# The passage into the FFN: a norm's sum of squares taken from sums per column block, and turns by diagonals

## The chip, the cores and the metric

One core of one Trainium2 chip runs the whole layer. Its engines are TensorE (PE: matmuls, with PEld for its weight loads), VectorE (DVE), ScalarE (ACT), GpSimd (POOL) and SyncE (SP, which issues most of the DMAs). The metric is the device time of one launch in microseconds (us); the median of three runs before the change is 1506.01 us (1505.78 to 1507.14).

## The reference

One transformer layer over 256 latent tokens and 256 context tokens of width 2048: attention in two kinds, merged by gates and an output projection, then a gated FFN with a short convolution. Between the two halves stand two norms, and these are what the change is about:

```python
def rms_norm(x, g):
    y = x * lax.rsqrt(jnp.mean(jnp.square(x), axis=-1, keepdims=True) + EPS)
    return y * g

y, yc = mixer_sublayer(...)                   # ends in "@ w_o"
x = x + gt1 * rms_norm(y, g_attn_post)        # first norm, gain, residual
h = modulate(rms_norm(x, g_ffn_pre), sh2, sc2)  # second norm, scale and shift
x = x + gt2 * rms_norm(conv_ffn(h, w_up, conv_w, conv_b, w_down), g_ffn_post)
```

Write y for the projection times its gain row, r1 for the first norm's factor and x for the layer's input. The new x is x + r1 y. The second norm needs the sum of (x + r1 y)^2 over the 2048 columns of each token, which is also r1^2 sum(y^2) + 2 r1 sum(xy) + sum(x^2).

## The kernel before

Everything is f32; large matmuls are made of three products of a high and a low part. Weights come in blocks of 128 x 2048 f32 (1024 KB) into one of four buffers named raw; ACT writes the high part (wh, L137), DVE the low part (wl, L141), and `block(3)` asks for the next block's parts and for the loads of three blocks further on. The kernel is written with a planner that orders the instructions of each engine by its own estimates; `issue_after(i)` places an instruction behind i on i's engine, and inside `manual_schedule` PE's order is that of the text.

The output projection is `norm_gain`: four column blocks c of 512, each over 16 row tiles, for the two token tiles t = 0, 1 (L913). In each of the first three column blocks four weight blocks g serve both t; in the last one, t=0 finishes first and t=1 last, each over two blocks of weights. `close(t)` takes the sum of squares of a finished block on ACT (L922) and multiplies by the gain row `grow` on DVE (L923). `extra`, here `beside(c, g)`, loads x1 (the layer's input, one half per token tile) and runs `mods`, products of modulation weights (raw<-in_wm_b) with a row `crb` on DVE (L234).

After the last block, `done(t)`, here `residual(t)`, runs. `rstd_tok` makes r1 from the sums (L952 to L955). DVE then writes x1 = yg * r1 + x1 in four blocks (L1018), and ACT squares each of them to get the second norm's sum (L1028). For t=1 the last block goes over PE instead: x1 times the identity (L1009), then yg times a diagonal matrix of r1 (L1015), both into px, which ACT squares. The second `rstd_tok` gives the second norm's factor.

Then the turns: h2, the FFN's input, is needed with features on the partitions. `turn(b, ts)` turns groups of one or two 128-column tiles through PE: group 0 is tile 0, group 1 tiles 1 and 2, up to group 8, tile 15. For t=0 in groups 0 to 3 it multiplies x1 by a diagonal of the second norm's factor (L1055), which turns and scales in one; all others are transposes (L1057) of tiles scaled beforehand by `scaled` (L998 on ACT, L999 on DVE). `split_h2(b)` applies scale and shift and writes the high and low halves of h2 (L1072 to L1078). `keep_busy(n)` puts n products of the identity with itself on PE (L266) as padding. The first four products of the FFN, `first_pairs`, run row tile by row tile among the turns (L1091, L1093, then L204 and L205). At the end x1 is stored to DRAM (L1138) for the layer's last residual.

Of the kernel before, what the change touches and what calls it, by code (L numbers as in the profile page):

```python
# [13 lines left out]
ALU = mybir.AluOpType  # L14
# [54 lines left out]
def layer_kernel(ctx, tc, xc, xt, ccol, crow, wm_sc, wm_sd, wm_sh, wm_b, cols, wk, wkt, ws, rope, mask_a, bias_b, out):  # L69
# [8 lines left out]
    def acc(name):  # L78
        return ps.tile([P, 512], F32, tag="a", bufs=6, name=name)
# [817 lines left out]

    final = []

    def norm_gain(act, nk, yg, grow, ss, nm, lead, done, extra=None):  # L900


        for c in range(4):
            py = [acc(f"py_{nm}{c}_{t}") for t in range(2)]
            cs = slice(c * 512, c * 512 + 512)

            def part(wts, g, t):
                wh, wl = wts
                for kk in range(4):
                    k = 4 * g + kk  # L910
                    w = slice(kk * 512, kk * 512 + 512)
                    for q, (a, wt) in enumerate(((0, wh), (1, wh), (0, wl))):
                        p_ = nc.tensor.matmul(  # L913
                            py[t][:], act[:, k, a, t * P : t * P + P], wt[:, w],
                            start=k == 0 and q == 0, stop=k == nk - 1 and q == 2)
                final[:] = [p_.ins]

            def close(t, after=None):
                with ExitStack() as es:
                    if after:  # L920
                        es.enter_context(tc.issue_after(after))
                    nc.scalar.activation(yg[:, t, cs], py[t][:], AF.Square, accum_out=ss[:, t, c : c + 1])  # L922
                nc.vector.tensor_tensor(out=yg[:, t, cs], in0=py[t][:], in1=grow[:, cs], op=ALU.mult)  # L923

            n = nk // 4
            for g in range(n if c < 3 else n - lead):
                wts = block(3)
                for t in range(2):
                    part(wts, g, t)
                if extra:  # L930
                    extra(c, g)
            if c < 3:
                for t in range(2):
                    close(t)
                if c == 1:
                    warm_table(AF.Sqrt, nm, ss[:, 0, 0:1])
            else:
                wts, after = [], None
                for g in range(n - lead, n):
                    wts.append(block(3))  # L940
                    part(wts[-1], g, 0)
                for t in range(2):
                    if t:
                        for i, g in enumerate(range(n - lead, n)):
                            part(wts[i], g, 1)
                    close(t, after)
                    after = done(t)
        return after

    def rstd_tok(ss, r):  # L950

        nc.vector.tensor_reduce(out=r, in_=ss[:, :3], axis=mybir.AxisListType.X, op=ALU.add)  # L952
        nc.vector.tensor_scalar(out=r, in0=r, scalar1=1.0 / D, scalar2=EPS, op0=ALU.mult, op1=ALU.add)
        a_ = nc.scalar.activation(r, ss[:, 3:4], AF.Sqrt, scale=1.0 / D, bias=r)
        v_ = nc.vector.reciprocal(r, r)  # L955
        return a_.ins, v_.ins
# [5 lines left out]
    with ExitStack() as ys:  # L962
# [1 line left out]
        x1 = yp.tile([P, 2, D], F32, name="x1")  # L964

        def beside(c, g):
            if g == 2 and c in (1, 2):
                sync.dma_start(out=x1[:, c - 1], in_=xt[:, c - 1])
            if c < 3 and g:
                mods(1, crb[:], (c, g) != (2, 3))  # L970
            if (c, g) == (2, 3):
                nc.vector.tensor_tensor(
                    out=modx[:, 16:48], in0=modx[:, 16:48], in1=col[:, C_BMOD + 48 : C_BMOD + 80], op=ALU.add)
                nc.vector.scalar_tensor_tensor(
                    out=gcol[:, 1, :], in0=modx[:, 32:48], scalar=1.0, in1=col[:, C_GPRE2 : C_GPRE2 + KT],
                    op0=ALU.add, op1=ALU.mult)

        yg = yp.tile([P, 2, D], F32, name="yg")
        grow = yp.tile([P, D], F32, name="grow")
        ss = yp.tile([P, 2, 2, 4], F32, name="ss")  # L980
        r = yp.tile([P, 2, 52], F32, name="r")

        crb = silu_row(yp)
        gain_row(0, grow)
# [1 line left out]

        pu, dg = [], {}

        def diagonal(n, t):

            dg[n] = yp.tile([P, P], F32, name=f"dg{n}")
            return nc.scalar.activation(dg[n][:], ident[:], AF.Copy, scale=r[:, n, t : t + 1]).ins

        def scaled(t, c0, c1, act=False):

            cs, r_ = slice(c0 * P, c1 * P), r[:, 1, t : t + 1]
            if act:
                return nc.scalar.activation(yg[:, t, cs], x1[:, t, cs], AF.Copy, scale=r_).ins  # L998
            return nc.vector.tensor_scalar(out=yg[:, t, cs], in0=x1[:, t, cs], scalar1=r_, scalar2=None, op0=ALU.mult).ins  # L999

        def residual(t):
            rstd_tok(ss[:, 0, t], r[:, 0, t : t + 1])
            c3 = slice(1536, 2048)
            if t:

                pu.extend(acc(f"pu0_{i}") for i in range(4))
                px = pu[3]
                with tc.issue_after(final[0]):
                    p_ = nc.tensor.matmul(px[:], ident[:], x1[:, t, c3], start=True, stop=False).ins  # L1009
                with tc.issue_after(p_):  # L1010
                    b_ = keep_busy(4, "2", pu[0])
                with tc.issue_after(diagonal(0, t)):
                    diagonal(1, 0)
                with tc.issue_after(b_):
                    p_ = nc.tensor.matmul(px[:], dg[0][:], yg[:, t, c3], start=False, stop=True).ins  # L1015
            for c in range(3 if t else 4):
                cs = slice(c * 512, c * 512 + 512)
                v_ = nc.vector.scalar_tensor_tensor(  # L1018
                    out=x1[:, t, cs], in0=yg[:, t, cs], scalar=r[:, 0, t : t + 1], in1=x1[:, t, cs],
                    op0=ALU.mult, op1=ALU.add)  # L1020
                s_ = ss[:, 1, t, c : c + 1]
                if t and c == 2:
                    with tc.issue_after(v_.ins):
                        v_ = nc.vector.scalar_tensor_tensor(
                            out=yg[:, t, cs], in0=x1[:, t, cs], scalar=1.0, in1=x1[:, t, cs],
                            op0=ALU.mult, op1=ALU.mult, accum_out=s_)
                else:
                    a_ = nc.scalar.activation(yg[:, t, cs], x1[:, t, cs], AF.Square, accum_out=s_)  # L1028
                if t and c == 0:
                    with tc.issue_after(a_.ins):  # L1030
                        a_ = nc.scalar.activation(yg[:, t, c3], px[:], AF.Square, accum_out=ss[:, 1, t, 3:4])
            if t == 0:
                rstd_tok(ss[:, 1, t], r[:, 1, t : t + 1])
                return a_.ins
            with tc.issue_after(v_.ins), tc.issue_after(a_.ins):
                return p_, rstd_tok(ss[:, 1, t], r[:, 1, t : t + 1])[0]

        p_, q_ = norm_gain(zz, KT, yg, grow, ss[:, 0], "o", 2, residual, beside)
        zs.close()


# [3 lines left out]
        def turn(b, ts, js=None):  # L1045

            if b not in ptx:
                ptx[b] = (acc if b % 2 else bank)(f"ptx{b}")
            for t in ts:
                for f, j in enumerate(group[b]):  # L1050
                    if js and j not in js:
                        continue
                    d = ptx[b][:, f * S + t * P : f * S + t * P + P]
                    if t == 0 and b < 4:
                        nc.tensor.matmul(d, x1[:, t, j * P : j * P + P], dg[1][:], start=True, stop=True)  # L1055
                    else:
                        nc.tensor.transpose(d, yg[:, t, j * P : j * P + P], ident[:])  # L1057

        def split_h2(b):
            with ExitStack() as es:  # L1060
# [35 lines left out]
        with tc.issue_after(p_), tc.manual_schedule(engines={mybir.EngineType.PE}):  # L1096
            for b in range(4):
                turn(b, (0,))
            keep_busy(8, "3", pu[0])

            a_ = nc.scalar.activation(x1[:, 1, 1536:], pu[3][:], AF.Copy)
            with tc.issue_after(a_.ins), tc.issue_after(q_):
                scaled(0, 7, 8, True)
                scaled(0, 8, 12, True)
            scaled(1, 0, 1)
            scaled(1, 1, 4)
            scaled(1, 4, 8)
            behind[:] = [scaled(1, 8, 12)]
            turn(0, (1,))
            split_h2(0)  # L1110
            turn(1, (1,))
# [7 lines left out]
            turn(3, (1,))  # L1119
            first_pairs(1)  # L1120
            split_h2(3)
            with tc.issue_after(behind[0]):
                behind[0] = scaled(0, 12, 16, True)
            with tc.issue_after(behind[1]):
                behind[1] = scaled(1, 12, 16)
            for k in range(2, KT):
                if k % 4 == 0:
                    wh, wl = parts[nblk[0]]
# [342 lines left out]
```

## Time and profile before

| | |
|---|---|
| median of the runs | 1506.01 us (1505.78 to 1507.14) |
| the profiled execution | 1505.69 us |
| its span | 1503.90 us |
| mean granted clock of TensorE | 0.999 |
| PE busy | 1492.0 us (99%) |
| DVE busy | 1202.0 us (80%) |
| ACT busy | 800.7 us (53%) |
| output projection, PE's L913 | 678.4 to 765.6 us of the span |
| turns, PE's L1055 and L1057 | 768.6 to 792.5 us of the span |

The span runs from the first to the last instruction of the profiled execution; 1.79 us of its time lie around it. A chain row gives the start, the length and what ran; a timeline row gives the start, the length, the engine, the line, the operation with its tiles, how many rows were merged, and in brackets the idle time before it and what ended that. A row of groups gives the durations of one in ns. DMA rows give the size and the us from issue to landing. Durations of matmuls overlap, since they are pipelined; how much time they occupy on PE is read from start to start, or from the chain.

### The profile page before, as it was taken

What the parts mean: (1) busy time and instruction counts of PE and PEld (TensorE: products, weight loads), DVE (VectorE), ACT (ScalarE), POOL (GpSimd) and SP (SyncE); (2) the same over time, 40 slices, a digit from 0 to 9 for tenths busy, and PEclk for the clock granted to TensorE, in tenths of its full rate; (3) what the DMA queues carried; (4) which work ended last, traced back from release to release, by engine and by line L of the source; (5) the groups of instructions that cost most, each with busy time, mean ns of one, the idle gap of its engine ahead of it and who ended that gap; (6) DMA issues with size and microseconds to landing.
All of it is one profiled execution on the core that took longest, in us unless ns stands there. A gap on an engine that the chain in (4) does not pass through costs nothing.

```text
span 1503.9 us, 21730 instructions
## 1 busy us (share of the span) xinstructions
PE 1492.0 (99%) x8513; PEld 1282.2 (85%) x8513; DVE 1202.0 (80%) x1797; ACT 800.7 (53%) x1309; POOL 1.6 (0%) x10
## 2 busy tenths in 40 slices
PE   9999999999999999999999999999999999999997
PEld 7876889898888888888888888888888888888886
DVE  4496897999988888877678887887888878777776
ACT  4342532777764554454467555555555565455443
POOL 0000000000000000000000000000000000000000
PEclk9999999999999999999999999999999999999999
DMA  9988779754468888878846666666766655645653
GB/s 366 396 322 335 278 285 343 275 171 167 142 229 299 321 322 324 299 278 323 348 182 217 247 237 237 244 236 221 252 228 234 213 194 179 241 174 194 234 238 112
DMA packets 59254, 381.08 MB, mean 253 GB/s; under 512 B 6544, under 2 KB 6928, under 8 KB 17040
## 3 DMA queue, kind: packets, MB, share of 16 engines
q1 hardware_dynamic: 58432, 378.63, 67.8%
q8 instruction: 67, 1.10, 0.3%
q10 hardware_dynamic: 720, 1.07, 0.2%
q14 instruction: 35, 0.29, 0.1%
HBM read 375.43 MB, written 4.24 MB: 252 GB/s over the span
## 4 chain that ended last, share of the span: by engine, by line
PE 97%; DMA 1%; DVE 1%; ACT 1%; issue 0%; DVEq 0%; ACTq 0%
PE pu L204 21%; PE c L1256 13%; PE pu L205 11%; PE pv L686 7%; PE pg L204 7%; PE pk L468 7%; PE py_o L913 6%; PE pq L204 4%; PE pb L204 4%; PE pg L205 4%; PE pq L205 2%; PE x L1256 2%; PE pb L205 2%; PE po L823 1%; PE s L793 1%; PE pm L342 1%
## 5 line engine op out<-in xcount | busy, mean ns | idle before, releaser
L141 DVE TENSOR_TENSOR wl<-raw,wh 128x1024 fp32r<-128x1024 f32 (+1 forms) x444 | 523.4, 1207 | 141.4 <-ACT wh L137 141.1
L137 ACT ACTIVATE wh<-raw 128x1024 fp32r<-128x1024 f32 (+1 forms) x444 | 446.5, 1041 | 221.8 <-PE c L1256 58.3
L204 PE MATMUL pu<-h,wh 128*128 128x512 f32 x1404 | 488.1, 391 | 0.0
L205 PE MATMUL pu<-h,wl 128*128 128x256 f32 x1404 | 395.9, 282 | 0.0
L204 PEld LDWEIGHTS pu<-h,wh 128*128 128x128 f32 x1404 | 263.6, 188 | 55.6 <-issue 0.4
L205 PEld LDWEIGHTS pu<-h,wl 128*128 128x128 f32 x1404 | 265.4, 189 | 0.0
L204 PE MATMUL pg<-h,wh 128*128 128x512 f32 x464 | 161.5, 390 | 0.0
L1256 PE MATMUL c<-wh,ff 128*128 128x512 f32 x512 | 158.1, 389 | 0.0
L205 PE MATMUL pg<-h,wl 128*128 128x256 f32 x464 | 130.8, 282 | 0.0
L234 DVE SCALAR_TENSOR_TENSOR raw<-raw,crb 128x2048 f32<-128x2048 f32 x48 | 109.7, 2286 | 12.5 <-DMA raw<-in_wm_b_dram 11.9
L468 PE MATMUL pk<-h,ku 128*128 128x512 f32 x480 | 118.1, 398 | 0.9 <-DVE ku L141 0.4
L1256 PEld LDWEIGHTS c<-wh,ff 128*128 128x128 f32 x512 | 96.1, 188 | 19.8
L209 ACT ACTIVATE half_u<-pu 128x256 f32<-128x256 f32 x88 | 33.5, 382 | 147.2 <-PE pu L205 147.2
L468 PEld LDWEIGHTS pk<-h,ku 128*128 128x128 f32 x480 | 87.5, 188 | 25.6 <-issue 4.8
L204 PE MATMUL pq<-h,wh 128*128 128x512 f32 x304 | 108.6, 395 | 0.0
L204 PEld LDWEIGHTS pg<-h,wh 128*128 128x128 f32 x464 | 87.1, 188 | 18.2
L686 PE MATMUL pv<-wh,h 128*128 128x512 f32 (+1 forms) x384 | 101.7, 354 | 0.0
L1256 PE MATMUL c<-wl,ff 128*128 128x512 f32 x256 | 99.8, 390 | 0.0
L204 PE MATMUL pb<-h,wh 128*128 128x512 f32 x256 | 89.4, 390 | 0.0
L205 PEld LDWEIGHTS pg<-h,wl 128*128 128x128 f32 x464 | 87.7, 189 | 0.0
L205 PE MATMUL pq<-h,wl 128*128 128x256 f32 x304 | 85.5, 281 | 0.0
L913 PE MATMUL py_o<-wh,zz 128*128 128x512 f32 x256 | 78.7, 389 | 0.0
(229 smaller groups left out, 2009.2 us busy)
## 6 DMA issues: line engine op xcount, KB each, us to landing
raw<-in_ws_dram SPq DMA_DIRECT2D x222, 1024.0 KB, 4.9
raw<-in_wm_b_dram SPq DMA_DIRECT2D x64, 1024.0 KB, 4.9
raw<-in_wm_sc_dram SPq DMA_DIRECT2D x15, 1024.0 KB, 8.0
raw<-in_wm_sh_dram SPq DMA_DIRECT2D x16, 768.0 KB, 6.3
raw<-in_wkt_dram SPq DMA_DIRECT2D x10, 1024.0 KB, 6.3
raw<-in_wk_dram SPq DMA_DIRECT2D x7, 768.0 KB, 8.5
crb<-sild SPq DMA_DIRECT2D x4, 1024.0 KB, 7.9
sd<-in_wm_sd_dram SPq DMA_DIRECT2D x4, 1024.0 KB, 7.6
```

What stands on the lines that cost most here:

```text
L137: a_ = nc.scalar.activation(hi, src, AF.Copy)
L141: v_ = nc.vector.tensor_tensor(out=lo, in0=src, in1=hi, op=ALU.subtract)
L204: nc.tensor.matmul(pt[:, :], wh[:, w], a, start=first and i == 0, stop=False, skip_group_check=True)
L205: nc.tensor.matmul(pt[:, :S], wl[:, w], a[:, 0], start=False, stop=last and i == n - 1, skip_group_check=True)
L209: a_ = nc.scalar.activation(t[:], pt[:, S:], AF.Copy)
L234: nc.vector.scalar_tensor_tensor(out=r, in0=r, scalar=1.0, in1=row, op0=ALU.mult, op1=ALU.mult, accum_out=modx[:, j : j + 1])
L342: nc.tensor.matmul(pm[32 * j : 32 * j + 32, t * P : t * P + P], cc[:, q, :], rsc[k + t][:, q * P : q * P + P], start=q < 4, stop=q >= KT - ...
L468: nc.tensor.matmul(pk[:], wt[:, w], hh[:, :, k, a], start=k == 0 and a == 0 and wt is wh, stop=k == KT - 1 and a == 1)
L686: nc.tensor.matmul(pv[i][:, :nw], src[:, k, a, t0 : t0 + P], wt[:, w], start=k == 0 and q == 0, stop=k == KT - 1 and q == 2)
L793: nc.tensor.matmul(s_ps[:], qs[hd][:, a, qt * P : qt * P + P], k_, start=q == 0, stop=q == 2)
L913: p_ = nc.tensor.matmul(py[t][:], act[:, k, a, t * P : t * P + P], wt[:, w], start=k == 0 and q == 0, stop=k == nk - 1 and q == 2)
L1256: nc.tensor.matmul(pt[:], a(i), wt[:, w], start=k not in begun, stop=stop and q == 2, skip_group_check=True)
```

## The change

The second norm's sum is no longer taken from the finished x1. `norm_gain` gets a hook `more(c, t, cs)`, called for every closed block. Here it is `sums`: ACT squares yg (y in the text above) into a scratch tile with an accumulated sum, DVE multiplies yg, 2 and x1 with an accumulated sum, and for c = 0, 1, 2 ACT also squares one or two blocks of x1. x1 is therefore loaded in the first column block, at g = 0 and 1, not in the second and third.

`residual(t)` then adds up the three sums, combines them with r1 in two Horner steps, clamps at zero, and makes the factor with `rstd_of`. Between these it places the first part of x1 (columns 0 to 128), then the diagonal `dg[t]` on ACT, then columns 128 to 512, then column blocks 1 and 2 for t=0 and block 1 for t=1. The remaining blocks (t=1 block 2, t=0 block 3, t=1 block 3) come on DVE after the split of turn group 3.

All turns are products with the diagonal of their t. The tiles are no longer scaled beforehand; the products into px are gone; the padding is 24 calls in one place instead of 4 and 8.

```diff
@@ norm_gain
                 nc.vector.tensor_tensor(out=yg[:, t, cs], in0=py[t][:], in1=grow[:, cs], op=ALU.mult)
+                if more:
+                    more(c, t, cs)
@@ beside
-            if g == 2 and c in (1, 2):
-                sync.dma_start(out=x1[:, c - 1], in_=xt[:, c - 1])
+            if c == 0 and g < 2:
+                sync.dma_start(out=x1[:, g], in_=xt[:, g])
@@ new helpers
+        def squared(t, cs, c):
+            nc.scalar.activation(junk[:, 0], x1[:, t, cs], AF.Square, accum_out=sq[:, t, 2, c : c + 1])
+
+        def sums(c, t, cs):
+            nc.scalar.activation(junk[:, 0], yg[:, t, cs], AF.Square, accum_out=sq[:, t, 0, c : c + 1])
+            nc.vector.scalar_tensor_tensor(
+                out=junk[:, 1], in0=yg[:, t, cs], scalar=2.0, in1=x1[:, t, cs], op0=ALU.mult, op1=ALU.mult,
+                accum_out=sq[:, t, 1, c : c + 1])
+            for q in range(c, c + 1 + c // 2) if c < 3 else ():
+                squared(t, slice(q * 512, q * 512 + 512), q)
+
+        def residual_part(t, a, b):
+            cs = slice(a, b)
+            return nc.vector.scalar_tensor_tensor(
+                out=x1[:, t, cs], in0=yg[:, t, cs], scalar=r[:, 0, t : t + 1], in1=x1[:, t, cs],
+                op0=ALU.mult, op1=ALU.add).ins
@@ residual(t), new body
+            r1, v = r[:, 0, t : t + 1], m[:, t, 3:4]
+            rstd_tok(ss[:, t], r1)
+            nc.vector.tensor_reduce(out=m[:, t, :3], in_=sq[:, t], axis=mybir.AxisListType.X, op=ALU.add)
+            for q in (1, 2):
+                nc.vector.scalar_tensor_tensor(
+                    out=v, in0=m[:, t, 0:1] if q == 1 else v, scalar=r1, in1=m[:, t, q : q + 1], op0=ALU.mult, op1=ALU.add)
+            v_ = nc.vector.tensor_scalar(out=v, in0=v, scalar1=0.0, scalar2=None, op0=ALU.max)
+            with tc.issue_after(v_.ins):
+                v_ = residual_part(t, 0, P)
+            with tc.issue_after(v_):
+                v_ = rstd_of(v, r[:, 1, t : t + 1])
+            dg[t] = yp.tile([P, P], F32, name=f"dg{t}")
+            a_ = nc.scalar.activation(dg[t][:], ident[:], AF.Copy, scale=r[:, 1, t : t + 1]).ins
+            with tc.issue_after(v_):
+                v_ = residual_part(t, P, 512)
+            for c in range(1, 3 - t):
+                with tc.issue_after(v_):
+                    v_ = residual_part(t, c * 512, c * 512 + 512)
+            if t == 0:
+                return a_
+            return final[0], v_
@@ turn
-                    if t == 0 and b < 4:
-                        nc.tensor.matmul(d, x1[:, t, j * P : j * P + P], dg[1][:], start=True, stop=True)
-                    else:
-                        nc.tensor.transpose(d, yg[:, t, j * P : j * P + P], ident[:])
+                    nc.tensor.matmul(d, x1[:, t, j * P : j * P + P], dg[t][:], start=True, stop=True)
@@ the turns and first products
             for b in range(4):
                 turn(b, (0,))
-            keep_busy(8, "3", pu[0])
...
-            behind[:] = [scaled(1, 8, 12)]
+            pu.extend(acc(f"pu0_{i}") for i in range(4))
+            keep_busy(24, "3", pu[0])
+            behind[:] = [q_]
             turn(0, (1,))
             split_h2(0)
...
             split_h2(3)
-            with tc.issue_after(behind[0]):
-                behind[0] = scaled(0, 12, 16, True)
-            with tc.issue_after(behind[1]):
-                behind[1] = scaled(1, 12, 16)
+            for t, c in ((1, 2), (0, 3), (1, 3)):
+                with tc.issue_after(behind[1]):
+                    behind[1] = residual_part(t, c * 512, c * 512 + 512)
```

More of the change, by code (lines that the diff above doesn't have):

```diff
@@ L898, in layer_kernel, with norm_gain @@
     final = []
-    def norm_gain(act, nk, yg, grow, ss, nm, lead, done, extra=None):
+    def norm_gain(act, nk, yg, grow, ss, nm, lead, done, extra=None, more=None):
         for c in range(4):
@@ L979, in layer_kernel @@
         grow = yp.tile([P, D], F32, name="grow")
-        ss = yp.tile([P, 2, 2, 4], F32, name="ss")
-        r = yp.tile([P, 2, 52], F32, name="r")
+        ss = yp.tile([P, 2, 4], F32, name="ss")
+        sq = yp.tile([P, 2, 3, 4], F32, name="sq")
+        r = yp.tile([P, 2, 2], F32, name="r")
+        m = yp.tile([P, 2, 4], F32, name="m")
+        yp.tile([P, 72], F32, name="rim3")
+        junk = yp.tile([P, 2, 512], F32, name="junk2")
         crb = silu_row(yp)
@@ L987, in layer_kernel @@
         pu, dg = [], {}
[L989 to L999, printed above, removed]
@@ L1001, in residual @@
-        def residual(t):
[L1002 to L1026, printed above, removed]
-                else:
[L1028 to L1031, printed above, removed]
-            if t == 0:
[L1033 to L1036, printed above, removed]
@@ L1038, in layer_kernel @@
-        p_, q_ = norm_gain(zz, KT, yg, grow, ss[:, 0], "o", 2, residual, beside)
+        def squared(t, cs, c):
[7 more added lines that the diff above has]
+                squared(t, slice(q * 512, q * 512 + 512), q)
@@ L1039, in layer_kernel @@
+        p_, q_ = norm_gain(zz, KT, yg, grow, ss, "o", 2, residual, beside, sums)
         zs.close()
@@ L1053, in turn @@
                     d = ptx[b][:, f * S + t * P : f * S + t * P + P]
-                    if t == 0 and b < 4:
-                        nc.tensor.matmul(d, x1[:, t, j * P : j * P + P], dg[1][:], start=True, stop=True)
-                    else:
-                        nc.tensor.transpose(d, yg[:, t, j * P : j * P + P], ident[:])
+                    nc.tensor.matmul(d, x1[:, t, j * P : j * P + P], dg[t][:], start=True, stop=True)
         def split_h2(b):
@@ L1098, in layer_kernel @@
                 turn(b, (0,))
-            keep_busy(8, "3", pu[0])
[L1101 to L1107, printed above, removed]
-            behind[:] = [scaled(1, 8, 12)]
+            pu.extend(acc(f"pu0_{i}") for i in range(4))
+            keep_busy(24, "3", pu[0])
+            behind[:] = [q_]
             turn(0, (1,))
```

## The prediction

> **What bounds the kernel now.** I read the page's shares of the chain that ended last, then the engines in four stretches, then the waits of PE and its weight loads (PEld), then the chain through the passage.
>
> ```profile
> PE 97%; DMA 1%; DVE 1%; ACT 1%; issue 0%; DVEq 0%; ACTq 0%
> 678.00:765.60 87.60, 87.60 (x389) 72.61 (x388) 61.29 (x71) 42.16 (x61) 0.00 (x0) 1.00 0.84 325
> 765.60:775.00 9.40, 8.71 (x62) 7.32 (x62) 7.13 (x19) 6.74 (x18) 0.00 (x0) 1.00 0.50 209
> 775.00:796.00 21.00, 21.00 (x125) 18.24 (x125) 17.30 (x31) 15.35 (x26) 0.00 (x0) 1.00 0.38 138
> 796.00:1500.00 704.00, 700.12 (x3723) 606.01 (x3721) 557.30 (x782) 385.23 (x574) 0.00 (x0) 1.00 0.60 218
> PE pu L1091 <- ACT h L1073: 0.4, 1, 0.4
> PEld pu L204 <- ACT h L1073: 0.2, 1, 0.2
> ```
>
> PE is the bound: 97% of the chain. A windows row gives the stretch, its length, then busy time of PE, PEld, DVE, ACT, POOL, the granted clock and the DMA share. In the output projection (678 to 765.6) PE is never idle, so nothing that is done sooner there can shorten the run; it can only become late. In the passage (765.6 to 775) PE idles 0.7 us. The clock is 1.00 throughout. From 796 on it is busy 700.1 of 704 us, and the waits view names no engine that it waits for there. So the change is worth what it does to PE's own list of work and waits between 765.6 and about 796, and a slip there reaches the end whole.
>
> The chain through the passage (start, length, what):
>
> ```profile
> 754.94 10.67 PE py_o L913 x47
> 765.63 0.70 ACT yg L922 x2
> ...
> 766.96 0.16 DVE r L955
> 767.14 0.41 ACT dg L992
> 767.60 1.12 PE pu L1015 x2
> 768.72 1.56 PE ptx L1055 x14
> 770.29 1.79 PE pu L266 x16
> 772.07 0.12 PE ptx L1057
> 772.22 0.57 ACT h L1073
> ...
> 774.96 0.26 PE pu L204
> ...
> 780.67 0.44 PE ptx L1057 x4
> ```
>
> The projection ends at 765.61, the first turn of t=1 at 772.19, and its first h2 tile starts on ACT at 772.22. PE passes 16 records of padding (8 calls of keep_busy: **two records a call**) right up to that turn. The real rows L204 begin at 774.96.
>
> ```profile
> L1057 PE MATMUL ptx<-ident,yg x25: 270/272/273, 771.9 to 792.5; 128*128 128x128 f32 x25
> L1055 PE MATMUL ptx<-dg,x x14: 273/275/275, 768.6 to 770.0; 128*128 128x128 f32 x14
> ```
>
> The code makes 25 transposes and 7 products with a diagonal: a transpose is one record, a product two. By the chain, a transpose occupies 0.44/4 = 0.11 us and a product 1.56/7 = 0.223 us.
>
> **The change part by part.**
>
> *Turns.* All 32 turns become products: 25 x (0.223 - 0.11) = 25 x 0.113 = 2.8 us more PE work, beside nothing, since PE has no idle time there. The Trainium skill, page "TensorE: Matmul & The Clock Gate", section Terms, says against this change that transpose mode is 4x faster for FP32. By that a product would be 0.44 us, the 25 turns would cost 8.2 us, and my total below would be near 10 us; the x14 row, at twice a transpose, decides against the 4, and the case gets no chance: those seven products have the same tiles and form.
>
> *Padding.* What leaves PE: the identity and diagonal products into px (L1009, L1015) and 12 calls of padding. What comes: 24 calls, 48 records of 1.79/16 = 0.112 us, 5.37 us. PE's list is written out by hand, so from 765.61: seven products for t=0, 1.56, to 767.17; padding to 772.54; first turn of t=1, two records, to **772.76, against 772.19: +0.57**. The seven need t=0's diagonal and columns up to 896, which are made beside the last 5.4 us of projection; these rows of DVE show the room:
>
> ```profile
> 760.91 0.69 DVE L923 TENSOR_TENSOR yg<-py_o,grow 128x512 f32<-128x512 f32 x1 [2.93 <-ACT yg L922]
> 761.71 2.74 DVE L1018 SCALAR_TENSOR_TENSOR x<-yg,r,x 128x512 f32<-128x512 f32 x4
> 762.49 0.64 ACT L1028 ACTIVATE yg<-x 128x512 f32<-128x512 f32 x1 [1.29 <-DVE x L1018]
> 763.03 0.18 ACT L1028 ACTIVATION_READ_ACCUMULATOR yg<-x 128x1 f32 x1
> 764.57 0.15 DVE L952 TENSOR_REDUCE r<-ss 128x1 f32<-128x3 f32 x1
> 764.76 0.15 DVE L953 TENSOR_SCALAR r<-r 128x1 f32<-128x1 f32 x1
> 765.56 0.16 DVE L955 RECIPROCAL r<-r 128x1 f32<-128x1 f32 x1 [0.65 <-ACT r L954]
> ```
>
> *The norm's chain for t=1.* ACT's square of the block ends at 766.33 (765.63 + 0.70) and the multiplication by the gain follows. The square of yg starts 0.78 us after that (as 761.71 to 762.49) and takes 0.72 with its read (762.49 to 763.21): 767.83. The sum, two Horner steps and the clamp go at 0.19 us each (764.57 to 764.76): the clamp issues near 768.5. Its reciprocal, with the root on ACT between, is at most 0.80 later (764.76 to 765.56, where ACT had a square to end first), the diagonal 0.18 and PE 0.46 after that (766.96, 767.14, 767.60): 769.9. The second norm is ready **2.6 us before the padding ends**: the shorter chain is real, and the padding stands in front of it. ACT and DVE follow the first turn, so their split of h2 is 0.57 us later too.
>
> *Up to turn group 4.* Groups 2 and 3 add four products, 0.45: L204 begins 1.02 later, at 775.98. The 0.2 us wait of PEld is taken up by that, some 0.16 of it: 0.86 late at 780.67, where group 4 starts: 781.53.
>
> *The new wait.* Group 4 turns columns 896 to 1152. Before, t=1's columns up to 1536 were scaled ahead of the first turn. Now residual_part(1, 1024, 1536) is put on DVE behind the split of group 3 (issue_after), where the last scaling, L999, stood (the last row is PE's, the others DVE's):
>
> ```profile
> 780.29 0.48 DVE L1078 SCALAR_TENSOR_TENSOR h<-ptx,gcol,h2t 128x256 fp32r<-128x256 f32 x1
> 781.79 0.48 DVE L1078 SCALAR_TENSOR_TENSOR h<-ptx,gcol,h2t 128x256 fp32r<-128x256 f32 x1
> 782.20 0.48 DVE L999 TENSOR_SCALAR yg<-x,r 128x512 f32<-128x512 f32 x1
> 780.92 0.47 PE L204 MATMUL pu<-h,wh 128*128 128x512 f32 x1
> ```
>
> It starts at 782.20 + 0.57 = 782.77, takes 2.74/4 = 0.69, and PE sees it 0.15 later (780.77 to 780.92): 783.61. PE has done three of the group's four turns by 782.2 and waits **1.4 us**; behind it in PE's queue stand the fourth turn and the rows of k=5, and ACT's split of group 4 waits for that turn. k=5 begins at 783.83 against 780.92: +2.9. I take this in full; its ends are 0 (the part issued early) and 1.4. The other two parts, 0.69 each, end near 784.9, ahead of group 6, and are free.
>
> *From k=5.* Groups 5 to 8 hold 14 turns: 14 x 0.113 = 1.58. DVE is then some 2 us late and PE 3, so the small waits of before (about 0.2) go. **Sum: 2.9 + 1.6 - 0.2 = +4.3 us.**
>
> *Sums per block.* 8 products on DVE (0.69) and 16 squares on ACT (0.72); those of the last block are in the chain above, the rest lies beside 87.6 us in which DVE is busy 61.3 and ACT 42.2. Cost 0; nothing to gain, PE being full. The bound above: four squares, 2.9 us, queued before a split of weights that has 1.6 us to spare (below), 1.3 us.
>
> *Loads of x1.* Two loads of 1024 KB move from the second and third column block to the first, on SP's queue among the weights. Cost 0 if SP issues them well ahead of grow, the row of the norm's gain; the other end is the third rival. The two stores of x1, on the same queue, now wait until about 785, behind which stand loads three blocks ahead of use: 0.
>
> The profiled execution took 1505.69 us, its span 1503.90. 1505.69 + 4.3 = 1509.99; the median shown, 1506.01, is 0.32 above that execution, so **1510.3**.
>
> **The rivals.**
>
> *No wait at group 4* (the part issued earlier, or DVE ahead of what I assume). Then 0.57 + 0.45 - 0.16 + 18 x 0.113 = +2.9: 1508.9. For it: DVE has gaps before 781.4; against it: the explicit order behind group 3's split.
>
> *The padding is short* (the other side: no measurable loss). Were a call of it one record, it would end at 767.17 + 2.69 = 769.86, just when the diagonal is ready; the first turn ends at 770.08, 2.1 sooner. DVE's part moves with it, k=5 starts at 781.15 (+0.2), and with 1.58 - 0.2 the total is +1.6: 1507.6. It decides from 2.7 us of padding downward. Against it: 16 records for 8 calls. Even this does not come out faster, because the products and DVE's part remain: with the wait at group 4 left out as well it is -2.1 + 0.45 + 2.0 = +0.4.
>
> *The x1 loads hold up the weights.*
>
> ```profile
> DMA packets 238, 1.69 MB, mean 422 GB/s; under 512 B 32, under 2 KB 32, under 8 KB 32
> raw<-in_wm_b_dram SPq DMA_DIRECT2D x1, 1024.0 KB, 8.6
> 687.61 0.33 SPq L130 DMA_DIRECT2D raw<-in_wm_b_dram  x1
> 696.92 2.28 DVE L234 SCALAR_TENSOR_TENSOR raw<-raw,crb 128x2048 f32<-128x2048 f32 x1
> 699.13 1.22 DVE L141 TENSOR_TENSOR wl<-raw,wh 128x1024 fp32r<-128x1024 f32 x1
> 701.96 0.39 PE L913 MATMUL py_o<-wl,zz 128*128 128x512 f32 x1
> ```
>
> At 422 GB/s each load takes 2.5 us. If both stand right behind grow, the modulation row issued at 687.61 lands at 701.2, not 696.2; DVE, holding it ahead of a split of weights, would finish that split at 704.6, and PE needs it at 701.96 (today 1.6 us to spare). Stall 2.7: +7.0, 1513.0. For it: that stretch moves data at the full rate. Against it: x1 lies in other memory than grow, which may come free sooner, and then both loads go ahead of that stretch.
>
> **How the numbers follow.** Chances: forecast 0.57, no wait 0.18, short padding 0.06, held weights 0.17, faster by something I do not see 0.02. The forecast and held weights lie above 1509.0, 0.2% over the median (about what a measurement of this kernel tells from no change), but for a 0.04 tail; the case at 1508.9 lies on that line, two thirds below. Slower 0.75, same 0.23, faster 0.02. The range, 1508.0 to 1513.2, takes in 1508.9 and 1513.0 and leaves out the short padding.
>
> **What would show it.** In the changed profile: 64 records of turns and no transposes; 48 records of padding ending near 772.5, with ACT's diagonal for t=1 done near 769.5 (2.6 us of padding behind it); one wait of PE for DVE's x of about 1.4 us near 782; no PE idle before 765.6. It would be wrong if that diagonal came after the padding, if the part for group 4 was there in time, or if PE idled in the projection.

## The result and the profile after

The changed kernel takes **1510.68 us** (median of 8 runs, 1509.71 to 1512.19) against 1505.88 us (1505.42 to 1507.14) for the kernel before on the same chip: a ratio of **1.0030, 95% interval 1.0021 to 1.0039**, slower by 3.2 to 5.9 us. Run again beside later experiments it gave 1510.57, ratio 1.0027 (1.0016 to 1.0038). The forecast was 1510.3. The profiled execution of the changed kernel took 1511.03 us, its span is 1509.3.

First the engines' shares of the chain that ended last, from the page of the changed kernel:

```profile
PE 90%; DVE 5%; DMA 3%; issue 1%; ACT 1%; SPq 0%; DVEq 0%; ACTq 0%
```

PE had 97% of this chain before, and DVE 1%. That is not 7% of standing still, since PE is busy for 99% of the span in both kernels: where PE waits for another engine even for a moment, the chain is followed back through that engine's list, beside which PE worked. So this row says that such a wait has come, and the windows say in which stretch PE stands still (length, then busy time of PE, PEld, DVE, ACT, POOL, clock, DMA):

```profile
678.00:765.60 87.60, 87.60 (x391) 72.57 (x390) 66.01 (x89) 49.77 (x84) 0.00 (x0) 1.00 0.84 324
765.60:775.00 9.40, 9.19 (x76) 8.80 (x75) 5.47 (x16) 3.32 (x9) 0.00 (x0) 1.00 0.00 0
775.00:796.00 21.00, 19.65 (x131) 17.83 (x130) 17.72 (x32) 13.27 (x22) 0.00 (x0) 1.00 0.54 202
```

The projection is as full as before (87.60 of 87.60). DVE's work in it rose from 61.29 to 66.01 us and ACT's from 42.16 to 49.77, the sums per block, at no cost to PE. From 765.6 to 775 PE idles less than before (0.21 against 0.69). In the stretch of the turns, from 775 to 796, it stands still for 1.35 us (21.00 less 19.65), where it stood still for none before, and the waits of PE name the reason:

```profile
PE ptx L1052 <- DVE x L1009: 1.4, 1, 1.4
PE s L793 <- DVE h L141: 1.1, 1, 1.1
```

The first row is the wait that the change brought. The second lies at 282 us, in attention, and is taken up below. Now the chain through the passage, to be held against the one in the prediction. All of this execution runs 1.29 us later than that one by the end of the projection (766.90 against 754.94 + 10.67 = 765.61), so differences of times are taken after subtracting that.

```profile
766.90 1.56 PE ptx L1052 x14
768.46 5.36 PE pu L266 x48
773.82 0.24 PE ptx L1052 x2
774.09 0.57 ACT h L1068
...
779.42 2.36 DVE wl L141 x2
...
782.15 0.50 DVE h L1073
782.67 0.57 ACT h L1068
...
783.65 0.48 DVE h L1073
784.13 0.67 DVE x L1009
784.85 0.49 PE ptx L1052 x2
```

Seven turns of t=0, 48 records of padding, then the first turn of t=1 at 773.82. From there to 784.13 the chain runs over ACT and DVE, not PE: the splits of h2 one after another, with a split of weights (L141) among them, end in the residual part for group 4 (L1009), and PE turns the last tile of that group only at 784.85. That t=1's factor was there long before is in the timeline of ACT and DVE (start, length, engine, line, operation, idle time before it):

```profile
766.94 0.60 ACT L922 ACTIVATE yg<-py_o 128x512 f32<-128x512 f32 x1 [1.37 <-PE py_o L913]
...
770.41 0.16 DVE L216 RECIPROCAL r<-r 128x1 f32<-128x1 f32 x1
770.61 0.40 ACT L1026 ACTIVATE dg<-ident,r 128x128 f32<-128x128 f32 x1 [0.23 <-DVE r L216]
774.68 0.35 DVE L1072 TENSOR_SCALAR h2t<-h,modx 128x256 f32<-128x256 f32 x1 [2.93 <-ACT h L1068]
```

The diagonal, the last step of t=1's norm on ACT, ends at 771.01, the padding at 773.82: 2.8 us of padding stand behind a finished norm, and DVE sits idle for 2.93 us in front of a split that cannot begin. The turns by form:

```profile
L1052 PE MATMUL ptx<-dg,x x64: 270/275/377, 766.7 to 798.0; 128*128 128x128 f32 x64
```

64 records for 32 turns; in the prediction's chain 7 such products and 25 transposes made 39.

**Where the time went.** I cut each profiled execution at three marks: the first and the last product of the projection, and the moment at which ACT's wait ends ahead of the last of the seven evacuations L209 that open the FFN, 0.06 us before that evacuation starts. The evacuations (before, then after):

```profile
L209 ACT ACTIVATE half_u<-pu x7: 361/372/386, 800.3 to 815.1; 128x256 f32<-128x256 f32 x7
```

```profile
L209 ACT ACTIVATE half_u<-pu x7: 362/373/384, 805.7 to 820.5; 128x256 f32<-128x256 f32 x7
```

The last product starts at 765.20 and 766.50, so the piece I call the passage takes 49.84 us before and 53.97 after: **+4.13**. The start of the projection moved from 678.38 to 679.63, +1.25; the projection itself took 86.83 and 86.87, the rest to the end 688.86 and 688.79. Together that is the 5.4 us between the spans (1503.9 and 1509.3). The table has the same pieces for every kernel that is spoken of here:

| kernel | median us (range, runs) | ratio, 95% interval | projection begins | projection | passage |
|---|---|---|---|---|---|
| before | 1505.88 (1505.42 to 1507.14, 8) | | 678.38 | 86.83 | 49.84 |
| after | 1510.68 (1509.71 to 1512.19, 8) | 1.0030, 1.0021 to 1.0039 | 679.63 | 86.87 | 53.97 |
| after, again | 1510.57 (1509.40 to 1512.28, 7) | 1.0027, 1.0016 to 1.0038 | 680.43 | 87.12 | 53.96 |
| padding 12 calls | 1507.41 (1506.88 to 1510.20, 11) | 1.0013, 1.0004 to 1.0022 | 680.81 | 87.31 | 51.46 |
| part for group 4 early | 1508.13 (1507.52 to 1509.83, 11) | 1.0015, 1.0006 to 1.0023 | 677.93 | 86.83 | 52.35 |
| both | 1506.50 (1505.39 to 1508.23, 11) | 1.0001, 0.9992 to 1.0010 | 679.55 | 86.84 | 49.83 |
| both, no padding | 1507.25 (1505.41 to 1510.41, 11) | 1.0007, 0.9998 to 1.0016 | 679.14 | 86.83 | 51.44 |
| both, transposes in groups 4 to 6 | 1505.81 (1504.97 to 1507.23, 11) | 0.9997, 0.9988 to 1.0006 | 678.51 | 87.97 | 48.99 |
| both, x1 loads apart | 1505.72 (1504.99 to 1508.97, 11) | 1.0001, 0.9992 to 1.0010 | 678.41 | 86.83 | 49.84 |
| both, loads apart, transposes in groups 4 and 5 | 1506.00 (1504.32 to 1508.05, 11) | 0.9999, 0.9990 to 1.0008 | 677.99 | 86.83 | 49.06 |
| before with the x1 loads moved | 1506.01 (1505.39 to 1507.66, 11) | 0.9998, 0.9989 to 1.0007 | 678.10 | 87.19 | 49.85 |
| before with loads and sums | 1507.34 (1505.86 to 1509.36, 11) | 1.0006, 0.9997 to 1.0015 | 680.04 | 87.04 | 49.86 |

Every ratio is to the kernel before, measured on the same chip beside that kernel (its medians there were 1505.88, 1505.97, 1505.86 and 1505.81). The last three columns are of one profiled execution each. A difference of medians is up to 1.5 us away from that of the passages, and in the profiles the projection begins anywhere from 677.9 to 680.8 us. So an edit of the passage is read from the passage, and the median says whether it lasts to the end.

### The profile page after: what moved, and what is told of

It is laid out like the page before. It is cut to its first block, busy times and chain, and to the rows that moved or that the text cites. A ratio compares the mean times of both kernels' runs of the same rounds, so it can differ in the third digit from the quotient of the medians.

```text
span 1509.3 us, 21850 instructions
## 1 busy us (share of the span) xinstructions
PE 1495.9 (99%) x8558; PEld 1287.0 (85%) x8558; DVE 1205.8 (80%) x1813; ACT 804.9 (53%) x1323; POOL 1.6 (0%) x10
## 4 chain that ended last, share of the span: by engine, by line
PE 90%; DVE 5%; DMA 3%; issue 1%; ACT 1%; SPq 0%; DVEq 0%; ACTq 0%
PE pu L204 21%; PE c L1243 13%; PE pu L205 11%; PE pk L468 7%; PE pg L204 7%; PE py_o L913 6%; PE pb L204 4%; PE pg L205 4%; PE pq L204 4%; PE x L1243 2%; PE pb L205 2%; PE pq L205 2%; DMA raw<-in_wm_b_dram 2%; PE po L823 1%; PE s L793 1%
## 5 line engine op out<-in xcount | busy, mean ns | idle before, releaser
L141 DVE TENSOR_TENSOR wl<-raw,wh 128x1024 fp32r<-128x1024 f32 (+1 forms) x444 | 523.3, 1206 | 136.4 <-ACT wh L137 135.9
L204 PE MATMUL pu<-h,wh 128*128 128x512 f32 x1404 | 487.7, 390 | 0.0
L205 PE MATMUL pu<-h,wl 128*128 128x256 f32 x1404 | 395.9, 282 | 0.0
L204 PEld LDWEIGHTS pu<-h,wh 128*128 128x128 f32 x1404 | 263.5, 188 | 55.1
L205 PEld LDWEIGHTS pu<-h,wl 128*128 128x128 f32 x1404 | 265.4, 189 | 0.0
L204 PE MATMUL pg<-h,wh 128*128 128x512 f32 x464 | 161.5, 390 | 0.0
L205 PE MATMUL pg<-h,wl 128*128 128x256 f32 x464 | 130.8, 282 | 0.0
L234 DVE SCALAR_TENSOR_TENSOR raw<-raw,crb 128x2048 f32<-128x2048 f32 x48 | 109.6, 2285 | 14.0 <-DMA raw<-in_wm_b_dram 13.4
L209 ACT ACTIVATE half_u<-pu 128x256 f32<-128x256 f32 x88 | 33.5, 382 | 146.9 <-PE pu L205 146.9
L204 PE MATMUL pq<-h,wh 128*128 128x512 f32 x304 | 108.6, 395 | 0.0
L204 PEld LDWEIGHTS pg<-h,wh 128*128 128x128 f32 x464 | 87.1, 188 | 18.2
L204 PE MATMUL pb<-h,wh 128*128 128x512 f32 x256 | 89.4, 390 | 0.0
L205 PEld LDWEIGHTS pg<-h,wl 128*128 128x128 f32 x464 | 87.7, 189 | 0.0
L205 PE MATMUL pq<-h,wl 128*128 128x256 f32 x304 | 85.5, 281 | 0.0
L210 DVE TENSOR_TENSOR u<-pu,half_u 128x256 f32<-128x256 f32 x88 | 37.0, 422 | 51.9 <-ACT half_u L209 51.8
```

Of the source, the lines that this page charges most:

```text
L141: v_ = nc.vector.tensor_tensor(out=lo, in0=src, in1=hi, op=ALU.subtract)
L204: nc.tensor.matmul(pt[:, :], wh[:, w], a, start=first and i == 0, stop=False, skip_group_check=True)
L205: nc.tensor.matmul(pt[:, :S], wl[:, w], a[:, 0], start=False, stop=last and i == n - 1, skip_group_check=True)
L209: a_ = nc.scalar.activation(t[:], pt[:, S:], AF.Copy)
L210: v_ = nc.vector.tensor_tensor(out=out_, in0=pt[:, :S], in1=t[:], op=ALU.add)
L234: nc.vector.scalar_tensor_tensor(out=r, in0=r, scalar=1.0, in1=row, op0=ALU.mult, op1=ALU.mult, accum_out=modx[:, j : j + 1])
```

## The experiments

The theory after the result was that of the prediction: the passage loses 4.1 us to three things, padding longer than the norm needs, one residual part that PE waits for, and 25 turns as products. The rivals were that the loss sits in one of them alone, or in the loads and sums of the projection.

**Half of the padding.** 24 calls of `keep_busy` become 12.

```diff
-            keep_busy(24, "3", pu[0])
+            keep_busy(12, "3", pu[0])
```

> The changed kernel with 12 calls of padding for 24. My theory: PE's own list sets the first turn of t=1, and the diagonal is ready 2.7 us before the padding ends; 24 records fewer at 0.112 us end it 2.7 us sooner, just when the diagonal is there. ACT's and DVE's split, and with it the late part of x1 that turn group 4 waits for, move along: 2.7 us less than the changed kernel, about 1508.0 us. Rival, the chain of the norm sets the turn: no change. Rival, the loss comes from the loads or the sums in the projection: no change.

The passage fell by 2.51 us, and the wait of PE for `x` remained. Its row among the waits of PE in this kernel:

```profile
PE ptx L1052 <- DVE x L1009: 1.4, 1, 1.4
```

The chain of this kernel through the passage:

```profile
770.08 2.68 PE pu L266 x24
772.76 0.42 PE ptx L1052 x2
```

24 records take 2.68 us, half of 5.36, and the first turn of t=1 follows with a record that is only 0.18 us late (0.42 for what took 0.24): that is all that is left of waiting for the diagonal. 2.68 less 0.18 is the 2.5 us gained. Everything behind moved forward by the same amount, the part for group 4 too, so the wait kept its size: DVE's list starts from the first turn, not from a fixed time. The median fell by 3.3; what goes beyond 2.5 does not come from the passage.

**The part for group 4 in its old place.** `residual` makes column block 2 for t=1 as it does for t=0, before the turns of t=1, while DVE is idle (the 2.93 us above).

```diff
-            for c in range(1, 3 - t):
+            for c in range(1, 3):
...
-            for t, c in ((1, 2), (0, 3), (1, 3)):
+            for t, c in ((0, 3), (1, 3)):
```

> The changed kernel with the part of x1 for t=1, columns 1024 to 1536, made before the first turn (DVE is idle for 2.9 us there) and not behind the split of group 3. My theory: the one wait of PE, 1.4 us in group 4, goes whole and nothing takes its place: about 1509.3 us. Rival, the wait only stands in front of another one (the split of h2 by DVE, which is nearly as late): less than 0.5 us.

The passage fell by 1.62 us and the wait is gone. The same place in the timeline of PE of this kernel:

```profile
780.81 0.28 PE L205 MATMUL pu<-h,wl 128*128 128x256 f32 x1
780.93 1.05 PE L1052 MATMUL ptx<-dg,x 128*128 128x128 f32 x8
781.74 0.48 PE L204 MATMUL pu<-h,wh 128*128 128x512 f32 x1
```

Group 4 now begins right behind the product before it and takes 0.81 us from start to start for its eight records, where the changed kernel waits 1.4 us ahead of its last two. The row that PE waited for was not late by itself: it stood on DVE behind the split of group 3. What disappears is 0.2 more than the wait. The median, 1508.13, lies 1.2 below what was expected; the projection of this profile begins 1.7 us sooner than the changed kernel's, which the edit does not order.

**Both edits.**

> Both: 12 calls of padding, and the part made before the first turn. If the two were independent, 4.1 us less than the changed kernel, 1506.6 us. DVE then makes that part (0.7 us) in front of its first split of h2, which would wait some 0.4 us for it: 1506.6 to 1507.0. The products instead of transposes remain and keep it at or above the kernel before.

The passage is 49.83 us against 49.84 before, 4.14 less than in the changed kernel and the sum of the two edits alone (2.51 + 1.62 = 4.13). The median is 1506.5, ratio 1.0001 (0.9992 to 1.0010): no difference from the kernel before. So the two edits take back the whole loss, although all 32 turns are still products. Its chain shows what pays for them:

```profile
766.78 1.56 PE ptx L1052 x14
768.35 2.68 PE pu L266 x24
771.03 0.42 PE ptx L1052 x2
...
773.29 0.44 PE ptx L1052 x4
```

The first turn of t=1 starts 4.25 us after the end of the projection, against 6.46 before (772.07 less 765.61): 2.2 us from the shorter norm, which the products use up by the last turn.

**No padding at all.** Both edits, and the call of `keep_busy` left out.

> As the last one, with no padding at all: PE idles some 2.5 us between the turns of t=0 and the diagonal of t=1. My theory, the diagonal sets the turn: the same as with 12 calls, within 0.3 us, and the granted clock stays 1.00. Rival, the padding keeps TensorE's clock up: a clock below 1.00 behind the gap, and 1 to 4 us more.

The passage got 1.61 us *longer* than with 12 calls, so it was the rival that held. PE stands idle for the diagonal, as it must (its timeline):

```profile
770.53 0.94 PE L1052 MATMUL ptx<-dg,x 128*128 128x128 f32 x6 [2.60 <-ACT dg L1026]
```

But the padding only filled that time. What is lost comes afterwards. The windows of this kernel, in which the third column from the end is the granted clock:

```profile
771.00:773.00 2.00, 1.79 (x14) 1.60 (x13) 1.89 (x5) 1.02 (x2) 0.00 (x0) 0.88 0.00 0
773.00:775.00 2.00, 2.00 (x11) 2.00 (x10) 1.23 (x3) 1.38 (x4) 0.00 (x0) 0.50 0.00 0
775.00:777.00 2.00, 2.00 (x11) 1.78 (x11) 1.82 (x5) 2.00 (x4) 0.00 (x0) 0.77 0.00 0
777.00:779.00 2.00, 2.00 (x13) 1.79 (x12) 2.00 (x3) 0.90 (x2) 0.00 (x0) 1.00 0.00 0
```

The clock falls to 0.50 some two microseconds after PE has begun to work again, and is back at 1.00 in the last window. From 771 to 777 the clock is short by 0.12, 0.50 and 0.23 of 2 us each, 1.7 us together, about the loss. In the kernel with 12 calls the same windows show 1.00. These are one profile each, but the mean granted clocks of the runs agree: 0.997 or 0.998 in the eleven without padding, 0.998 or 0.999 in the eleven with 12 calls. The medians lie only 0.75 apart, and their ranges overlap. The chain of the kernel without padding shows what it does to a turn:

```profile
773.08 0.85 PE ptx L1052 x4
773.93 0.85 PE pu L1088 x4
```

Four records take 0.85 us, at full clock 0.44 (the last row of the chain with both edits). So the padding earns its place by the clock, and 12 calls are enough for that; no number between 0 and 12 was run. The Trainium skill, page "TensorE: Matmul & The Clock Gate", section "What's actually happening", puts the fall of the clock after about 3.4 us of idle time; here an idle time of 2.6 us was followed by it, and the measurement decides.

**The projection's part, put into the kernel before.** First the x1 loads alone, then the loads and the sums for the first three column blocks, whose results nothing reads (the norm is still taken from the finished x1).

```diff
-            if g == 2 and c in (1, 2):
-                sync.dma_start(out=x1[:, c - 1], in_=xt[:, c - 1])
+            if c == 0 and g < 2:
+                sync.dma_start(out=x1[:, g], in_=xt[:, g])
```

> The kernel before with nothing changed but the two loads of x1, moved to the first column block. My theory: they cost nothing, since PE has no wait in the projection of the changed kernel either, though ACT waits there for weights: within 0.5 us of the kernel before, the projection 86.8 us on PE. Rival, the loads hold up weights: PE idles up to 2.7 us in the projection.

> The kernel before with the loads moved and the three sums of column blocks 0 to 2 taken as in the change, their results unused. My theory: the 6 products on DVE and 14 squares on ACT lie beside the projection: within 0.5 us of the last one, the projection 86.8 us. Rival, they push a split of weights past its time: up to 1.3 us more.

With the loads alone the median is 1506.01, ratio 0.9998; the passage is untouched (49.85), the projection 87.19 against 86.83. With the sums it is 1507.34, ratio 1.0006 (0.9997 to 1.0015), projection 87.04, passage 49.86. Neither makes the 4 us. The second median lies 1.3 us above the first. Between their profiles the difference is mostly ahead of the projection, which begins at 680.04 against 678.10.

In the changed kernel 1.1 of the 1.25 us of that early piece are the second wait in the list above, from 282.0 to 283.1 us; with loads and sums it is there too, 1.3 us. The chain leads from it back to a row of DVE which holds for a load; this is that row before, and then after:

```profile
262.04 2.29 DVE L234 SCALAR_TENSOR_TENSOR raw<-raw,crb 128x2048 f32<-128x2048 f32 x1 [0.96 <-DMA raw<-in_wm_b_dram]
```

```profile
263.52 2.29 DVE L234 SCALAR_TENSOR_TENSOR raw<-raw,crb 128x2048 f32<-128x2048 f32 x1 [3.41 <-DMA raw<-in_wm_b_dram]
```

DVE waits 3.41 us there, not 0.96, and its row starts 1.48 us later. The next load of weights goes out as much later, and a split of h some 19 us behind makes PE wait 1.1. Up to the projection each engine has the same instructions in the same order in all these kernels, and the projection begins at 677.93 in one and at 680.81 in another of those that differ from the changed kernel only behind it. Single runs of the kernel before reach 1508.9 too. Why the load comes late more often in some of the kernels stays open; no run here tests it.

**Transposes where there is room.** The version with both edits, with turn groups 4 to 6 as transposes again: ACT scales their tiles, in three gaps between the splits of groups 1, 3 and 5.

```diff
-                    nc.tensor.matmul(d, x1[:, t, j * P : j * P + P], dg[t][:], start=True, stop=True)
+                    if b in (4, 5, 6):
+                        nc.tensor.transpose(d, yg[:, t, j * P : j * P + P], ident[:])
+                    else:
+                        nc.tensor.matmul(d, x1[:, t, j * P : j * P + P], dg[t][:], start=True, stop=True)
...
+        ahead = {1: (7, 9), 3: (9, 11), 5: (11, 13)}
...
+                if f and b in ahead:
+                    after = a_.ins
+                    for t in range(2):
+                        with tc.issue_after(after):
+                            after = scaled(t, *ahead[b])
```

> The version with 12 calls of padding and the early part, with turn groups 4 to 6 as transposes again; their tiles are scaled by ACT in three of its gaps. My theory: 12 products fewer by 0.113 us each on PE, 1.4 us less than that version: the passage 48.5 us for 49.8, about 1505.1 us. Rival, PE is not the bound there but the split of h2 by ACT and DVE is, which the scalings lengthen: no gain or a loss.

The passage is 0.84 us shorter than with both edits alone, not 1.36 (12 x 0.113). Group 4 goes as worked out; its timeline on PE:

```profile
780.15 0.60 PE L1053 MATMUL ptx<-ident,yg 128*128 128x128 f32 x4
780.50 0.48 PE L204 MATMUL pu<-h,wh 128*128 128x512 f32 x1
...
785.20 0.76 PE L1053 MATMUL ptx<-ident,yg 128*128 128x128 f32 x4
785.71 0.48 PE L204 MATMUL pu<-h,wh 128*128 128x512 f32 x1
...
787.07 0.28 PE L205 MATMUL pu<-h,wl 128*128 128x256 f32 x1
787.44 0.51 PE L204 MATMUL pu<-h,wh 128*128 128x512 f32 x1
787.78 0.28 PE L205 MATMUL pu<-h,wl 128*128 128x256 f32 x1
787.90 0.39 PE L204 MATMUL pu<-h,wh 128*128 128x512 f32 x1
```

0.35 us from start to start, where the eight records of products took 0.81: 0.46 for four turns, 0.115 each. Of the 0.52 us that is missing, 0.16 goes in group 6, whose four turns take 0.51 from start to start: its third turn follows the end of ACT's last scaling for that group. The other 0.36 goes at 787.44: that L204 starts 0.37 us after the L205 before it, the next one 0.12, and it takes 0.34 to its own successor, where the others take 0.23. The chain leaves PE for DVE there:

```profile
784.18 2.35 DVE wl L141 x2
...
786.90 0.49 DVE h L1091
787.44 0.51 PE pu L204
```

The product waits for a split of h2 that stood on DVE behind a split of weights. So the rival holds for these 0.36 us. PE's projection took 87.97 us in this profile, 1.1 more than in the kernel before, which the next experiment takes up. The median is 1505.81, ratio 0.9997 (0.9988 to 1.0006).

**The loads apart, and the best of all this.** The two loads of x1 go to row blocks 1 and 3 of the first column block; the second kernel adds transposes in groups 4 and 5 alone.

```diff
-            if c == 0 and g < 2:
-                sync.dma_start(out=x1[:, g], in_=xt[:, g])
+            if c == 0 and g % 2:
+                sync.dma_start(out=x1[:, g // 2], in_=xt[:, g // 2])
```

> The shortened padding and the early part of x1 stay (as in the kernel with both edits, 1506.5); the two loads of x1 are put beside row blocks 1 and 3 of the first column block, not 0 and 1, so that they no longer stand together right behind grow. Theory (the two loads together crowd the weights in some executions, 0.2 to 1.1 us): the projection from its first to its last product takes 86.8 us with no hesitation of PE between 700 and 721 us, and the median falls by 0 to 0.5 us, to 1506.0 to 1506.5. Rival (the hesitations have another cause, or come from the number of bytes in that stretch, not from where the loads stand): 87.0 to 87.9 us as before, median 1506.5. A third way: the second load now lands later than the squares of x in the first column block want it, ACT is held there, and the projection loses 1 us or more.

> Both edits, the loads of x1 apart, and transposes instead of products in turn groups 4 and 5 alone (group 6 lost about 0.5 us when its tiles were scaled on ACT). Theory: the passage takes 8 x 0.113 = 0.9 us less than with both edits alone, 48.9 us, the projection 86.8, and the run is 0.5 to 1 us under the kernel before: 1505.0 to 1505.5, within what a measurement tells from no change. Rival (the loss in group 6 was no matter of its scaling): 49.4 us and no gain over the kernel before.

Both projections take 86.83 us, with no hesitation. Of the nine profiles with the loads side by side, five took 87.04 to 87.97 and four 86.83 to 86.87, so that two short ones in a row come by chance about one time in five. That speaks for the theory and doesn't prove it, and the medians show nothing of it: 1505.72 and 1506.00, ratios 1.0001 and 0.9999. The passage of the second is 49.06, 0.77 less than with both edits (0.9 was expected), so the 12 transposes of the version before it were worth no more than these 8 within 0.1 us.

No version beats the kernel before by more than a measurement can tell: the best medians of this table lie within 0.2 us of its own.

**The changed kernel again.**

> The changed kernel itself once more, on this chip with the others. My theory: passage 54.0 us as in its first profile, 4.1 more than before; what its first profile lost ahead of the projection (1.25 us) is a chance delay of loads and differs here: 1509.7 to 1511.0 us. Rival, that part belongs to the change: the projection begins 1.2 us later again.

1510.57 us, passage 53.96: the piece repeats to 0.01 us, while its projection begins 0.8 later and takes 0.25 longer than in the first profile. The early piece did differ, as the theory has it, but it was late again, 2.05 us behind the kernel before, so this run does not decide between the theory and its rival.

## Why the prediction was right

It was right in sign, size and place. The forecast for the passage was +4.3 us; it measured +4.13. The medians differ by 4.8 and the profiled executions by 5.3. In the profiled ones what goes beyond 4.13 arises ahead of the projection, most of it in a wait of which the prediction knew nothing and which the change does not order; for the medians that is not shown. So the closeness of 1510.3 to 1510.68 owes some tenths of a microsecond to chance. That a slip of the passage reaches the end whole held: the rest behind it takes 688.86 us before and 688.79 after. By its own steps:

- *Turns.* 64 records and no transposes, as forecast. The price of 0.113 us a turn held: 0.115 in group 4 of the experiment with transposes, so a product is twice a transpose here, not four times.
- *Padding.* 48 records in 5.36 us (forecast 5.37). The first turn of t=1 begins at 773.82, 6.92 us after the projection's end in the chain; forecast 772.54 after 765.61, 6.93. It ends at 774.06, 7.16 after the projection against 6.58 before: +0.58, forecast +0.57.
- *The norm's chain.* The diagonal was to be seen by PE 4.3 us after the projection's end, 2.6 ahead of the padding's; it ended on ACT at 4.11, 2.8 ahead. The kernel without padding shows when PE takes it up: 4.16 us after the projection's end (770.53 less 766.37). Halving the padding gained 2.5.
- *The new wait.* 1.4 us forecast and 1.4 found, in the group and on the engine and line named. PE's timeline at its end:

```profile
784.85 0.49 PE L1052 MATMUL ptx<-dg,x 128*128 128x128 f32 x2 [1.35 <-DVE x L1009]
785.09 0.48 PE L204 MATMUL pu<-h,wh 128*128 128x512 f32 x1
```

The first product of k=5 (L204) begins at 785.09 after and at 780.92 before, 2.9 us later when the 1.29 are taken off, as forecast. Taking the wait away gained 1.62.
- *From k=5.* 1.58 less 0.2, 1.4, was forecast; 4.13 less 2.9, 1.2, came. This is the term that was sized too large, by some 0.15 us. PE's timelines show which part it is. From start to start the turns of groups 5 to 8 take 0.81, 0.81, 0.81 and 0.36 us, against 0.35, 0.36, 0.36 and 0.14 before: 1.59 more in all, as forecast. The real products between them take 0.29 less, and the rest up to the mark 0.06 less: 0.35 of small waits went, not 0.2.
- *Sums per block.* Cost 0 was forecast; the projection takes 0.04 us longer in the first profile of the changed kernel and 0.2 with loads and sums alone, at the price of 4.7 us of DVE and 7.6 of ACT beside it.
- *Loads of x1.* The forecast of no cost held, but **not for the reason given**. It asked that SP issue both loads well ahead of grow; the timeline of SP shows the place that the third rival named, right behind it:

```profile
685.66 0.42 SPq L260 DMA_DIRECT2D grow<-ggd  x1
686.13 0.90 SPq L970 DMA_DIRECT2D x<-in_xt_dram  x2
688.86 0.33 SPq L130 DMA_DIRECT2D raw<-in_wm_b_dram  x1
```

The load of the modulation row behind them did come as late as the rival said: it landed 13.8 us after its issue, not 8.6. The rival's 2.7 us of stall needed one thing more, that DVE hold the modulation row ahead of the second half of a split of weights, as it stood before. In the changed kernel the planner has put both halves first (DVE's timeline):

```profile
697.03 2.36 DVE L141 TENSOR_TENSOR wl<-raw,wh 128x1024 fp32r<-128x1024 f32 x2 [0.82 <-ACT wh L137]
...
703.67 2.29 DVE L234 SCALAR_TENSOR_TENSOR raw<-raw,crb 128x2048 f32<-128x2048 f32 x1
```

Both halves run from 697.03 in one piece, and the modulation row (L234) comes at 703.67, so the late load holds up neither of them. What was argued against the rival (x1's memory may come free sooner) was wrong; as far as the traces go, its fall rests on the order of two instructions that the change did not mention, and that the loss stayed away was luck in this respect. No run here has the loads side by side and the old order, so that the order is what saved it is argued, not shown. In small the rival's mechanism may be there: five of the nine projections with the loads side by side are longer, by up to 1.1 us.

Of the rivals, *no wait at group 4* and *short padding* are each refuted by the trace, and the two experiments that make them true bring 1.6 and 2.5 us, where the rivals reckoned with 1.4 and 2.7.

## What to carry to other kernels

A shorter chain earns nothing until the work put in front of its consumer is shortened with it: padding written for the old chain has to be sized again. Here half of it was enough to keep the clock, and none cost 1.6 us; what lies between was not run. When work is deferred behind another engine's list, look for the consumer's place in the order, not at the engine's idle time: 2.93 us of idle DVE stood ten microseconds before the row that PE waited for. And a piece cut by marks in the trace repeated to 0.01 or 0.02 us here, where single runs of one kernel lie up to 3 us apart and more.

## What the runs showed of the hardware

In the one profile of the kernel without padding, an idle time of PE of 2.6 us, with a second one of 0.2 us a microsecond after it, was followed by a fall of the granted clock to 0.50; with 2.7 us of padding in its place the clock stayed at 1.00. The fall came some two microseconds after PE had resumed and took 1.7 us of full-speed work from the next 6 us, so that 2.6 us of idle time which cost nothing by themselves made the passage 1.6 us longer behind them.
